# SSD group-norm factors: broadcast to all partitions by two DMAs through DRAM in place of products with the identity

## The chip, the core and the metric

The kernel runs on one core of one Trainium2 chip. The metric is the device time of one execution in microseconds (us). Three executions of the kernel before took 2750.94, 2751.69 and 2755.02 us; their median is 2751.69 us.

## The reference

The program is a two-layer decoder trunk on 1040 positions (16 learned meta tokens and 1024 inputs) of width 1024. Layer 0 mixes with an RG-LRU and an S5, layer 1 with a Mamba-2 SSD; each is followed by a squared-ReLU MLP. The change lies in the SSD mixer of layer 1, in the norm over each of its 8 groups of 256 channels:

```python
def ssd_mixer(h, w_in, conv_w, conv_b, dt_bias, a_log, d, norm_w, w_out):
    proj = h @ w_in
    z = proj[..., :SSD_INNER]
    ...
    y = ssd_chunked(xs, dt, a, bm, cm) + d.astype(jnp.float32)[:, None] * xs
    g = y.reshape(bsz, t, SSD_INNER) * jax.nn.silu(z.astype(jnp.float32))
    g = g.reshape(bsz, t, SSD_GROUPS, -1)
    g = g * lax.rsqrt(jnp.mean(g * g, axis=-1, keepdims=True) + NORM_EPS)
    g = g.reshape(bsz, t, SSD_INNER) * norm_w.astype(jnp.float32)
    return g.astype(dtype) @ w_out
```

## The kernel before

Activations are held with channels on the 128 partitions and tokens on the free axis, in three token tiles: 384, 384 and 256 tokens in the SSD's output (`TL`), and 16 more in the first one ahead of it. Every large product is made of three TensorE passes on parts of the operands (`mm3`, L182 to L184), into PSUM tiles `mm`, of which there are 4; small products go to 4 PSUM tiles `sm`.

The SSD stage works on the 8 groups one after the other (`mixer1`, loop over g). For each group it runs over 9 chunks of tokens, c from 0 to 8. `ssd_s1` transposes a chunk (L1358), makes the score product (L1372) and turns a loaded decay tile `csb` into weights (L1376 on ACT, L1378 on POOL); `ssd_s2` makes the chunk's output in an `mm` tile (L1389, L1392) and the next state (L1396), and DVE finishes the output into `zs` (L1412 to L1418). Between the steps of a chunk TensorE is given other products: the input projections of the next group (`proj`: evacuated by ACT at L1267, then by DVE at L1264, L1272 and L1274, or L1285 to L1290 for the gates) and the output projections of earlier token tiles (`wout`: DVE adds each result to `h`, L1471).

After the chunks 3, 6 and 8 the token tile i = 0, 1 or 2 is complete, and `ssd_norm` (L1421) is added to a list of generators that `step` moves on. It has these parts:

- ACT squares both halves of the tile, POOL adds them.
- `token_sums`: for each chunk of 128 tokens a product with a column of ones (L253) leaves the sums with tokens on partitions, and DVE makes the factor 1/sqrt(mean + eps) by a bit trick and three Newton steps (L258, L193 to L198). The result is `rsy`, 128x3 for a tile of 384 tokens and 128x2 for one of 256; its last step is an L198.
- `token_bcast` (L270): for each chunk a product of the factors with the identity writes them to all partitions, on the free axis, in the `sm` tile. Each of these products stands as two rows in the trace. There are 3 of them for i = 0 and 1, and 2 for i = 2, 8 a group.
- DVE multiplies both halves of `zs` by the norm's weights and the factors (L1443), ACT casts the result to `yh` (L1455), DVE makes the rest `yl` (L1456). `yh` and `yl` are what `wout` multiplies.

The engines work each in the order of their own queue. That order is set when the program is built, by a scheduler that takes instructions by priority as their inputs become ready; the table `SHIFT` (L64) shifts the priority of some functions, in this stage of `token_sums` and `load_w`. SP's queue issues the DMAs of the stage in its order: weights `wraw` (three buffers), decay tiles `csb` and `ecb` (three buffers each).

Of the kernel before, what the change touches and what calls it, by code (L numbers as in the profile page):

```python
# [10 lines left out]
F32 = mybir.dt.float32  # L11
# [7 lines left out]
P = 128  # L19
# [59 lines left out]
class Trunk:  # L79
# [1341 lines left out]
    def ssd_norm(self, pg, g, i):  # L1421

        nc = self.nc
        v = nc.vector
        o, w = TL[i]
        y = self.prod[g, "z", i]
        m = o - TT[i][0]
        acc, sq = (self.prod[g, k, i][:, m:m + w] for k in ("x0", "x1"))
        nc.scalar.activation(out=acc, in_=y[:, 0], func=AF.Square)
        nc.scalar.activation(out=sq, in_=y[:, 1], func=AF.Square)  # L1430
        nc.gpsimd.tensor_tensor(out=acc, in0=acc, in1=sq, op=ALU.add)
        yield
        yield
        sums = self.token_sums([acc], w, 256, self.sm())
        yield
        if i == 0:
            self.flush()
            self.wo[g] = [self.load_w(self.A["ssd_out"][2 * g + j], pg, "o", lo_pool=(j == 1)) for j in range(2)]
        wo = self.wo[g]
        yield  # L1440
        rb = self.token_bcast(sums, w)
        for j in range(2):
            v.scalar_tensor_tensor(out=y[:, j], in0=y[:, j], scalar=self.col("gnorm", 2 * g + j), in1=rb, op0=ALU.mult, op1=ALU.mult)  # L1443
        if g == 7 and i != 1:

            pool, q, wt = ((self.px, "xbc0", 400), None, (pg, "xbc1", 384))[i]
            yh, yl = ([pool.tile([P, wt], F32R, name=q, bufs=6) for _ in range(2)] for _ in range(2))
            for j in range(2):
                nc.scalar.copy(yh[j][:, :w], y[:, j])
                v.tensor_tensor(out=yl[j][:, :w], in0=y[:, j], in1=yh[j][:, :w].bitcast(F32), op=ALU.subtract)  # L1450
        else:
            self.flush(8)
            yh = pg.tile([P, 2, 384], F32R, name="yh", bufs=2)
            yl = pg.tile([P, 2, 384], F32R, name="yl", bufs=2)
            nc.scalar.copy(yh[:, :, :w], y)  # L1455
            v.tensor_tensor(out=yl[:, :, :w], in0=y, in1=yh[:, :, :w].bitcast(F32), op=ALU.subtract)  # L1456
            yh, yl = ([q[:, j] for j in range(2)] for q in (yh, yl))
        yield
        self.wq += [(g, wo, (yh, yl), i, n) for n in range(KT)]
# [252 lines left out]
```

## Time and profile before

| | |
|---|---|
| median of three executions | 2751.69 us |
| the profiled execution | 2751.07 us |
| its span in the trace | 2749.3 us |
| TensorE (PE) busy, whole span | 2664.6 us, 97% |
| VectorE (DVE) busy | 1963.5 us, 71% |
| ScalarE (ACT) busy | 1076.9 us, 39% |
| GpSimd (POOL) busy | 1034.7 us, 38% |
| SSD stage with its eight groups | 1163 to 2060 us of the span |

The profiled execution stands 0.6 us under the median of the runs. Times of instructions are read from its trace, in us from the start of the span. A busy PE is a pipelined one: its rows overlap, and the cost of a row is the time from its start to the start of the next one. Idle time of an engine that isn't the bound costs nothing by itself.

### The profile page before, as it was taken

How to read it: one execution, taken by the hardware profiler on the slowest of the kernel's cores; microseconds unless marked ns; L12 is line 12 of the kernel's file. 1: busy time of each engine (PE TensorE's matmuls, PEld its weight loads, DVE VectorE, ACT ScalarE, POOL GpSimd, SP SyncE). 2: the span in 40 equal slices, each digit the busy share in tenths (PEclk: the TensorE clock that was granted, in tenths of full speed). 3: DMA queues.
4: the chain of work that ended last, by engine and by line, in shares of the span. 5: the costliest groups of instructions: out<-in, count | busy, mean ns of one | idle time of the engine just before them, and what ended most of it. 6: DMA issues, size and time to landing. Idle time of an engine off the chain costs nothing.

```text
span 2749.3 us, 44507 instructions
## 1 busy us (share of the span) xinstructions
PE 2664.6 (97%) x17121; PEld 2551.6 (93%) x17121; DVE 1963.5 (71%) x3877; ACT 1076.9 (39%) x2207; POOL 1034.7 (38%) x842
## 2 busy tenths in 40 slices
PE   7998999999999999999999999999989999999998
PEld 7887999999999999899999999998988999999998
DVE  9887465666666686876767767677786666666685
ACT  5565344233233233453434434344454333333334
POOL 2122115454444532142233322333444554554542
PEclk9989999999999999999999999999999999999999
DMA  4422411111111110121211212123311111111111
GB/s 165 112 76 57 148 47 47 47 54 43 51 51 47 51 39 29 44 94 59 69 62 60 76 59 69 62 60 97 109 55 64 54 51 50 54 50 50 47 43 62
DMA packets 117909, 176.35 MB, mean 64 GB/s; under 512 B 13376, under 2 KB 47936, under 8 KB 117568
## 3 DMA queue, kind: packets, MB, share of 16 engines
q1 hardware_dynamic: 117408, 173.34, 20.3%
q8 instruction: 135, 2.21, 0.3%
q14 instruction: 78, 0.64, 0.1%
q10 hardware_dynamic: 288, 0.15, 0.0%
HBM read 158.34 MB, written 8.72 MB: 61 GB/s over the span
## 4 chain that ended last, share of the span: by engine, by line
PE 51%; DVE 6%; ACT 1%; DMA 1%; POOL 1%; issue 0%; DVEq 0%; ACTq 0%; POOLq 0%; SPq 0%
PE mm L182 12%; PE mm L183 12%; PE mm L184 12%; PE pd L182 3%; PE pd L184 3%; PE pd L183 3%; DVE xbc L1272 1%; PE mm L1392 1%; PE sm L1396 1%; PE mm L1389 1%; PE sm L1358 1%; DMA csb<-csd 1%; PE sm L253 1%; PE sm L270 0%; PE sm L1372 0%
## 5 line engine op out<-in xcount | busy, mean ns | idle before, releaser
L182 PE MATMUL mm<-hi,whi 128*128 128x384 f32 (+4 forms) x3120 | 1019.0, 327 | 16.1 <-ACT whi L176 8.6
L183 PE MATMUL mm<-lo,whi 128*128 128x384 f32 (+4 forms) x3120 | 1007.5, 323 | 0.9 <-DVE lo L300 0.5
L184 PE MATMUL mm<-hi,wlo 128*128 128x384 f32 (+4 forms) x3120 | 1004.2, 322 | 2.3 <-POOL wlo L177 2.3
L182 PEld LDWEIGHTS mm<-hi,whi 128*128 128x128 f32 x3120 | 591.0, 189 | 26.0 <-ACT whi L176 9.4
L183 PEld LDWEIGHTS mm<-lo,whi 128*128 128x128 f32 x3120 | 590.9, 189 | 7.2 <-DVE lo L300 0.8
L184 PEld LDWEIGHTS mm<-hi,wlo 128*128 128x128 f32 x3120 | 592.5, 190 | 3.3 <-POOL wlo L177 3.0
L182 PE MATMUL pd<-pc 128*128 128x260 f32 (+1 forms) x1176 | 377.0, 321 | 6.3 <-DVE s L375 2.2
L184 PE MATMUL pd<-pc 128*128 128x260 f32 (+1 forms) x1176 | 374.7, 319 | 0.0
L183 PE MATMUL pd<-pc 128*128 128x260 f32 (+1 forms) x1176 | 373.6, 318 | 0.0
L492 DVE TENSOR_TENSOR h<-h,pd 128x520 f32<-128x520 f32 (+1 forms) x336 | 291.8, 870 | 59.6 <-PE pd L184 45.2
L375 DVE SCALAR_TENSOR_TENSOR s<-mm,rb 128x384 f32<-128x384 f32 (+2 forms) x192 | 98.6, 514 | 265.1 <-PE mm L184 252.2
L389 POOL TENSOR_TENSOR pc<-ca,pc 128x512 fp32r<-128x512 f32 x112 | 169.8, 1516 | 244.8 <-ACT pc L388 164.1
L389 POOL TENSOR_TENSOR pc<-draw,pc 128x512 fp32r<-128x512 f32 x84 | 125.1, 1489 | 338.2 <-ACT pc L388 338.2
L182 PEld LDWEIGHTS pd<-pc 128*128 128x128 f32 x1176 | 221.5, 188 | 22.1 <-DVE acc L492 4.5
L184 PEld LDWEIGHTS pd<-pc 128*128 128x128 f32 x1176 | 221.6, 188 | 15.9
L183 PEld LDWEIGHTS pd<-pc 128*128 128x128 f32 x1176 | 221.6, 188 | 12.5
L176 ACT CAST whi<-wraw 128x512 fp32r<-128x512 f32 x286 | 167.6, 616 | 164.1 <-PE mm L183 150.2
L376 ACT ACTIVATE sq<-s 128x384 f32<-128x384 f32 (+2 forms) x192 | 94.1, 490 | 347.1 <-DVE s L375 347.0
L492 DVE TENSOR_TENSOR acc<-acc,pd 128x520 f32<-128x520 f32 (+1 forms) x234 | 190.3, 861 | 4.2 <-PE pd L184 4.1
L177 DVE TENSOR_TENSOR wlo<-wraw,whi 128x512 fp32r<-128x512 f32 x224 | 167.0, 764 | 18.1 <-ACT whi L176 9.4
L1378 POOL TENSOR_TENSOR csb<-csb,sc 128x512 f32<-128x512 f32 x64 | 89.7, 1402 | 210.3 <-DVE sc L1374 199.1
L388 ACT CAST pc<-cb 128x520 fp32r<-128x520 f32 (+1 forms) x112 | 70.0, 625 | 247.2 <-PE pd L184 130.4
(390 smaller groups left out, 4531.6 us busy)
## 6 DMA issues: line engine op xcount, KB each, us to landing
wraw<-in_mlp_up SPq DMA_DIRECT2D x128, 256.0 KB
wraw<-in_ssd_in SPq DMA_DIRECT2D x120, 256.0 KB
draw<-in_mlp_down SPq DMA_DIRECT2D x112, 256.0 KB
csb<-csd SPq DMA_DIRECT2D x64, 256.0 KB
ecb<-ecd SPq DMA_DIRECT2D x128, 64.0 KB
wraw<-in_ssd_out SPq DMA_DIRECT2D x32, 256.0 KB
wraw<-in_ev_in SPq DMA_DIRECT2D x24, 256.0 KB
wraw<-in_ev_out SPq DMA_DIRECT2D x18, 256.0 KB
```

The costliest lines, as they stand in the source:

```text
L176: nc.scalar.copy(h, raw)
L177: e.tensor_tensor(out=l, in0=raw, in1=h.bitcast(F32), op=ALU.subtract)
L182: nc.tensor.matmul(pt, lhsT=whi, rhs=xhi, start=first, stop=False)
L183: nc.tensor.matmul(pt, lhsT=whi, rhs=xlo, start=False, stop=False)
L184: nc.tensor.matmul(pt, lhsT=wlo, rhs=xhi, start=False, stop=last)
L253: nc.tensor.matmul(st[:l, 508 + i:509 + i], lhsT=a[:, o:o + l], rhs=self.ones, start=j == 0, stop=j == len(accs) - 1)
L375: nc.vector.scalar_tensor_tensor(out=r, in0=pt[:, :w], scalar=0.0, in1=rbs[i], op0=ALU.max, op1=ALU.mult)
L376: nc.scalar.activation(out=dst[:, o - t0:o - t0 + w].bitcast(F32), in_=r, func=AF.Square)
L388: nc.scalar.copy(hi, x)
L389: e.tensor_tensor(out=lo, in0=x, in1=hi.bitcast(F32), op=ALU.subtract)
L492: v.tensor_tensor(out=d, in0=d, in1=src, op=ALU.add)
L1378: nc.gpsimd.tensor_tensor(out=csb, in0=csb, in1=sc.unsqueeze(1).broadcast_to([P, 4, P]), op=ALU.mult)
```

## The change

For the first seven groups the products of `token_bcast` are left out. The factors are stored by one DMA into a tile in DRAM, so that the 128 tokens of a chunk lie one behind the other there (the store's elements are 4 bytes each), and a second DMA reads this row of 384 or 256 factors back into all 128 partitions of an SBUF tile `rbg`, of which there is one. The last group keeps the products. Lines behind L1434 stand 9 lines lower in the changed kernel: L1443 is L1452 there, L1455 is L1464, L1456 is L1465, L1471 is L1480.

```diff
         sums = self.token_sums([acc], w, 256, self.sm())
+        if g < 7:
+
+            st, y1, ch = sums
+            fd = self.dr.tile([3, P], F32, name=f"fd{g}{i}")
+            n = len(ch)
+            nc.sync.dma_start(fd[:n].rearrange("c p -> p c"), y1)
+            rb = pg.tile([P, 384], F32, name="rbg", bufs=1)[:, :w]
+            nc.sync.dma_start(rb, fd[:n].rearrange("c p -> (c p)").unsqueeze(0).broadcast_to([P, w]))
         yield
         if i == 0:
             self.flush()
             self.wo[g] = [self.load_w(self.A["ssd_out"][2 * g + j], pg, "o", lo_pool=(j == 1)) for j in range(2)]
         wo = self.wo[g]
         yield
-        rb = self.token_bcast(sums, w)
+        if g == 7:
+            rb = self.token_bcast(sums, w)
```

SP's queue has 42 more DMAs, 21 stores (L1440) and 21 loads (L1442). In the third group it reads, from the norm of the first tile to that of the third:

```order
L174 DMA wraw<-in_ssd_in 128x512 x2
L1440 DMA fd_15334<-rsy 128x3x1
L174 DMA wraw<-in_ssd_in 128x512 x2
L1442 DMA rbg<-fd_15334 128x384
L1341 DMA csb<-csd 128x512
...
L1344 DMA ecb<-ecd 64x2x128 x2
L1440 DMA fd_15800<-rsy 128x3x1
L174 DMA wraw<-in_ssd_in 128x512
L1442 DMA rbg<-fd_15800 128x384
L174 DMA wraw<-in_ssd_in 128x512
L1341 DMA csb<-csd 128x512
...
L1440 DMA fd_16135<-rsy 128x2x1
L1442 DMA rbg<-fd_16135 128x256
```

For i = 0 and 1 loads of weights stand between the store and the load back; for i = 2 the load back is the next in the queue, and so waits there for the store.

On DVE the products with the factors move forward. In the third group's second norm (i = 1) the queue before reads, from the last evacuation of a projection's tile 2 on:

```order
L1274 SCALAR_TENSOR_TENSOR xbc_15703<-s_15704,xbc_15703 128x256
L1272 SCALAR_TENSOR_TENSOR xbc_15764<-mm,cols,xbc_15764 128x399
L1412 TENSOR_TENSOR ty<-mm,ecb 128x256
...
L1274 SCALAR_TENSOR_TENSOR xbc_15764<-s_15765,xbc_15764 128x400
L1418 TENSOR_TENSOR zs_14956<-zs_14956,ty 128x2x128
L1272 SCALAR_TENSOR_TENSOR xbc_15830<-mm,cols,xbc_15830 128x384 x3
L1264 TENSOR_TENSOR s_15865<-mm,rb_11522 128x260
L1443 SCALAR_TENSOR_TENSOR zs_14803<-zs_14803,cols,sm 128x384 x2
```

and that of the changed kernel, from the same instruction on:

```order
L1274 SCALAR_TENSOR_TENSOR xbc_15712<-s_15713,xbc_15712 128x256
L1452 SCALAR_TENSOR_TENSOR zs_14809<-zs_14809,cols,rbg 128x384 x2
L1465 TENSOR_TENSOR yl<-zs_14809,yh 128x768
L1272 SCALAR_TENSOR_TENSOR xbc_15773<-mm,cols,xbc_15773 128x399
L1412 TENSOR_TENSOR ty<-mm,ecb 128x256
```

The two products and the rest `yl` now stand ahead of the evacuation of the first tile of the next projection. In the third norm (i = 2) they move in the same way, from behind the L1418 of the last chunk to ahead of the L1374:

```order
L1290 SCALAR_TENSOR_TENSOR zs_16112<-s_16113,zs_16112 128x384
L1480 TENSOR_TENSOR h<-h,mm 128x384 x2
L1452 SCALAR_TENSOR_TENSOR zs_14966<-zs_14966,cols,rbg 128x256 x2
L1465 TENSOR_TENSOR yl<-zs_14966,yh 128x2x256
L1374 TENSOR_TENSOR sc<-sm,tri 128x128
```

In the first norm (i = 0) the products stand some three instructions earlier. TensorE's queue is the same up to the end of the seventh group but for the products that are left out; there some 64 of its instructions change places.

## Rows read from the trace of the kernel before

**Rows 1.** The page, busy time of TensorE over the span.
```profile
PE 2664.6 (97%) x17121; PEld 2551.6 (93%) x17121; DVE 1963.5 (71%) x3877; ACT 1076.9 (39%) x2207; POOL 1034.7 (38%) x842
```
**Rows 2.** Busy time by windows: span, then busy us of each engine, PEclk, DMA.
```profile
1424.00:1538.00 114.00, 113.69 (x767) 109.38 (x766) 82.21 (x202) 46.38 (x108) 35.75 (x34) 1.00 0.22 65
```
**Rows 3.** Waits of PE, 1200 to 1960: us in total, times, longest.
```profile
PE mm L1389 <- DVE h L1471: 4.6, 6, 1.5
...
PE mm L183 <- DVE yl L1456: 0.8, 4, 0.3
```
**Rows 4.** Line L270, 1160 to 2060: duration ns, and who waited for it.
```profile
L270 PE MATMUL sm<-ident,rsy x134: 270/275/421, 1221.1 to 2048.5; 128*128 128x128 f32 x134
...
  DVE zs L1443: 11.5, 13
```
**Rows 5.** Timeline of PE, third group, i = 1: start, us, instruction.
```profile
1488.19 0.83 PE L270 MATMUL sm<-ident,rsy 128*128 128x128 f32 x6
1488.86 0.49 PE L1358 MATMUL sm<-ident,xbc 128*16 128x128 f32 x3
1489.10 0.42 PE L182 MATMUL mm<-hi,whi 128*128 128x384 f32 x1
```
**Rows 6.** Timeline of PE, third group, i = 2.
```profile
1523.38 0.61 PE L270 MATMUL sm<-ident,rsy 128*128 128x128 f32 x4
1523.74 0.36 PE L182 MATMUL mm<-hi,whi 128*128 128x256 f32 x1
```
**Rows 7.** Timeline of SP in layer 0: a store to DRAM and its load.
```profile
271.86 2.59 SPq L871 DMA_DIRECT2D yd<-s5yg  x4
276.50 0.33 SPq L877 DMA_DIRECT2D s5y<-yd  x1
```
**Rows 8.** Timeline of ACT in layer 0: the first reader of that load.
```profile
279.81 0.95 ACT L884 ACTIVATE s<-s5y 128x400 f32<-128x400 f32 x2 [0.49 <-DMA s5y<-yd]
```
**Rows 9.** The page, DMA queues: packets, MB, share of 16 engines.
```profile
q1 hardware_dynamic: 117408, 173.34, 20.3%
```
**Rows 10.** Timeline of SP, third group, around the norms i = 0 and 1.
```profile
1437.14 6.54 SPq L174 DMA_DIRECT2D wraw<-in_ssd_in  x4
...
1474.99 3.18 SPq L174 DMA_DIRECT2D wraw<-in_ssd_in  x2
```
**Rows 11.** Timeline of DVE, third group, i = 1; in brackets the idle time before.
```profile
1473.83 0.16 DVE L198 SCALAR_TENSOR_TENSOR rsy<-rst,rsy 128x3 f32<-128x3 f32 x1
...
1477.73 0.42 DVE L1274 SCALAR_TENSOR_TENSOR xbc<-s,xbc 128x256 f32<-128x256 f32 x1
1480.74 0.63 DVE L1272 SCALAR_TENSOR_TENSOR xbc<-mm,cols,xbc 128x399 f32<-128x399 f32 x1 [2.59 <-ACT xbc L1267]
...
1483.70 0.90 DVE L1274 SCALAR_TENSOR_TENSOR xbc<-s,xbc 128x400 f32<-128x400 f32 x1 [0.41 <-ACT s L1273]
...
1486.66 1.93 DVE L1272 SCALAR_TENSOR_TENSOR xbc<-mm,cols,xbc 128x384 f32<-128x384 f32 x3 [1.73 <-ACT xbc L1267]
```
**Rows 12.** Timeline of DVE, third group, i = 2.
```profile
1509.46 0.16 DVE L198 SCALAR_TENSOR_TENSOR rsy<-rst,rsy 128x2 f32<-128x2 f32 x1
...
1512.24 0.55 DVE L1471 TENSOR_TENSOR h<-h,mm 128x384 f32<-128x384 f32 x1 [0.16 <-PE mm L184]
1517.02 0.29 DVE L1374 TENSOR_TENSOR sc<-sm,tri 128x128 f32<-128x128 f32 x1 [4.22 <-PE sm L1372]
```
**Rows 13.** Timeline of DVE, third group, i = 0.
```profile
1441.04 0.15 DVE L198 SCALAR_TENSOR_TENSOR rsy<-rst,rsy 128x3 f32<-128x3 f32 x1
...
1450.03 1.92 DVE L1272 SCALAR_TENSOR_TENSOR xbc<-mm,cols,xbc 128x384 f32<-128x384 f32 x3
```
**Rows 14.** Line L1443, 1160 to 2060: duration ns min/median/max.
```profile
L1443 DVE SCALAR_TENSOR_TENSOR zs<-zs,cols,sm x48: 473/605/615, 1222.7 to 2049.2; 128x384 f32<-128x384 f32 x32, 128x256 f32<-128x256 f32 x16
```
**Rows 15.** Line L1272 with operands in SBUF alone, 1160 to 1960.
```profile
L1272 DVE SCALAR_TENSOR_TENSOR xbc<-s,cols,xbc x78: 462/478/1516, 1160.5 to 1836.5; 128x256 f32<-128x256 f32 x78
```
**Rows 16.** Busy time by windows, in the last group's tail.
```profile
1998.80:2012.50 13.70, 11.05 (x44) 9.13 (x44) 11.21 (x33) 5.05 (x13) 5.85 (x7) 0.50 0.09 28
```

## The prediction

> **What bounds the kernel now.** I read the page first. TensorE is busy for 97% of the span and no other engine comes near it [rows 1]: read from this row that DVE, ACT and POOL have a fourth or more of the time to spare on average. Then I read windows of one group of the SSD stage each, since an average says nothing of a stage. In the third group's window TensorE is busy 113.69 of 114.00 us at a granted clock of 1.00 (the upper level, 2.4 GHz), DVE 82.21 [rows 2]. So here a product that is left out shortens the path, as long as nothing else becomes late. The waits of TensorE say the same: its largest, for DVE's additions to `h`, are 4.6 us in six places over 760 us, and those for the rest `yl` are 0.8 us [rows 3]. Last I read the places of the change on TensorE, DVE and SP.
>
> **What is removed.** The trace has 134 rows of L270 in the stage, about 275 ns each [rows 4]. They overlap, so I price them by starts. At i = 1 the three products are six rows from 1488.19, and the next instruction starts at 1488.86: 0.67 us [rows 5]. At i = 2 the two products start at 1523.38 and the next instruction at 1523.74: 0.36 us [rows 6]. With i = 0 like i = 1, a group loses 2 x 0.67 + 0.36 = 1.70 us, and seven groups lose **11.9 us**. The L1443 behind them waited for L270 for 11.5 us [rows 4], but on DVE, which has time; I count nothing for that.
>
> **What is added: the two DMAs.** Their landing is not in the trace of before, so I bound it. The nearest row is the bounce in layer 0, where 128-partition rows are stored to `yd` and loaded back. Four stores take 2.59 us to issue from 271.86, so the last begins near 273.9; the load is issued at 276.50, 2.6 us later [rows 7]; its first reader starts at 279.81, 3.3 us later, having waited for that DMA [rows 8]. One bounce is then 2.6 + 3.3 = **5.9 us** from the factors to the readers. This is the low end. The change stores single elements of 4 bytes, 384 of them. The page gives 117408 packets on the main queue at 20.3% of 16 engines over 2749.3 us [rows 9], so 0.203 x 16 x 2749.3 / 117408 = 0.076 us for a packet of 1.5 KB on average. If each element is a packet and they are spread over 16 engines, 24 packets add 1.8 us (7.7 us in all); if one engine takes them all, 29 us are added (35 us in all). I take 5.9 to 7.7, since the same queue spreads all its other work, and keep 35 as the far end. The Trainium skill ("DMA: Bandwidth & Descriptors", section "Rules for kernel authors") speaks against such a store: a non-contiguous last dimension is lowered to one descriptor per element, and should be rearranged. No row here shows a store of that kind; by that rule the bounce is the 7.7 or the 35 above, not the 5.9.
>
> **What the bounce delays.** *SP.* At i = 0 and 1 the queue has weight loads around these moments (1437.14 for 6.54 us, 1474.99 for 3.18 us [rows 10]), and the new order puts one or two between store and load back, which covers most of the store's landing. What stands behind, `csb`, comes later by two issues of about 0.33 us each [rows 7]; TensorE has no wait for `csb` among those above 0.3 us. I count nothing.
>
> *DVE, i = 0.* Factors at 1441.2, DVE at the products near 1450.0 [rows 13]: 8.8 us, more than 7.7. No wait.
>
> *DVE, i = 1.* Factors at 1474.0. The moved L1452 stands behind the L1274 that ends at 1478.15. DVE was idle there for 2.59 us anyway, until 1480.74 [rows 11]. With 5.9 us `rbg` lands at 1479.9: DVE waits 1.8 us. Then come two products (0.605 us each [rows 14]), ACT's cast and DVE's rest. These two are as wide as both products together; I take 1.2 us each. So the evacuation of the next projection tile (L1272) starts at 1479.9 + 3.6 = 1483.5 in place of 1480.74, 2.8 us late. DVE's gaps of 0.41 and 1.73 us right behind [rows 11] take 2.1 us of it. TensorE doesn't feel it before it needs that tile's `mm` buffer again. There are four: this tile, the output tile of the chunk, the next two projection tiles; the fifth begins at 1489.10 [rows 5]. The tile's readers were done by 1483.3 (the start of L1274 less its gap of 0.41 [rows 11]), so 5.8 us of delay are free. **The limit:** L1272 may start at 1486.5, `rbg` may land at 1482.9, and the bounce may take 8.9 us.
>
> *DVE, i = 2.* Factors at 1509.6, DVE at the moved products at 1512.8; it idled 4.22 us there, until 1517.02 [rows 12]. With 5.9 us `rbg` lands at 1515.5. Products, cast and rest on two thirds of the width take 2.4 us, so the L1374 at 1517.02 starts 0.9 us late. I assume the limit of i = 1 here too. In return `yl` is ready some ten microseconds before `wout` wants it, so the 0.8 us of waits for it [rows 3] may go.
>
> *DVE's own time.* L1443 read PSUM and now reads SBUF alone. Such an L1272 of 256 columns takes 478 ns in the median, as L1443's shortest (473), but up to 1516 [rows 14, 15]. The cost over 42 instructions lies between nothing and 42 x 1.0 = 42 us, near the median by far, on an engine idle for 32 of 114 us a group. It is hidden by those gaps; without them it would be TensorE's.
>
> **Sum.** The profiled execution took 2751.07 us, 0.6 under the median of the runs. 2751.07 - 11.9 = 2739.2; against the median 2739.8. I forecast **2740 us**.
>
> **Rivals.**
> 1. *The gain is given back in small waits or in the tail.* For: late evacuations at i = 1 end within 0.7 us of what the gaps take; TensorE already waits for DVE's L1471 six times [rows 3]; in the end of the seventh group some 64 instructions of TensorE change places; and the last group has a stretch of 13.70 us at a granted clock of 0.50 (the lower level, 1.2 GHz), in which TensorE was busy 11.05 us [rows 16]. Were that stretch half as long again, 13.7 / 2 x 0.5 = 3.4 us would go; 0.5 us at each of 14 norms gives back 7. Together 10.4, or a time near 2750; with either alone 2743 to 2747. Against: the four `mm` buffers. Within 0.2% (5.5 us) of before, 2746 to 2757: 17%.
> 2. *Slower: the element store makes the bounce longer than the limit.* DVE stands still in its queue at L1452, no `mm` tile is evacuated, and TensorE stops. Each microsecond over 8.9 costs up to one at each of the 14 norms with i = 1 and 2. The change loses from 8.9 + 11.9 / 14 = 9.8 us on. A bounce of 12 us gives 3.1 x 14 - 11.9 = +31, 2783 us; one engine for all elements (35 us) would give 26.1 x 14 - 11.9 = +353, 3105 us. For: no row shows so fine a store. Against: 384 elements are little work when spread. 12%. The skill's rule above is this rival's first step: by it alone, with the packets spread, the sum stays.
> 3. *More gain.* DVE's norm work moves forward, PSUM's `sm` tile is free sooner, and TensorE's waits of 4.6 and 0.8 us [rows 3] vanish: 2740 - 5.4 = 2734.6 us. Part of the faster cases, 12%.
> 4. *The removed products were hidden.* If TensorE had been waiting at those places, nothing would be gained. The rows before and behind are back to back [rows 5, 6], so I give it no share of its own beyond the first rival.
>
> **How the numbers follow.** About 0.2% is what a measurement of this kernel can tell from no change. Forecast with its near misses (2736 to 2746): 59%; more gain: 12%; so faster 71%, same 17%, slower 12%. The range leaves out the slower rival and the far end of the others: 2734 (all waits gone) to 2750 (both give-backs).
>
> **What would show it.** Right: 112 rows of L270 fewer in the stage; a group's period shorter by 1.7 us; DVE waits of one to three microseconds for `rbg` at i = 1 and fewer or none at i = 0; no new wait of TensorE above a microsecond. Wrong: from the readiness of the factors to the start of L1452 more than 9 us; new waits of TensorE for L1272 or L1471 at i = 1 or 2; SP late with `csb`, seen as waits of TensorE for POOL's L1378; a longer stretch at 0.50 in the last group.

## The result and the profile after

The changed kernel took 2918.59 us (median of five executions, 2915.51 to 2921.41) beside 2751.6 us before: a ratio of 1.0606, with a 95% interval of 1.0594 to 1.0617. It is **167 us slower** where 12 us less were forecast. The profiled execution has a span of 2913.8 us. One of the eight executions of e15 below took 6615.55 us in a slower state and is left out of its time.

The page of the changed kernel: busy time, then the chain of work that ended last by engine and by line.

```profile
PE 2693.8 (92%) x17009; PEld 2574.2 (88%) x17009; DVE 1974.7 (68%) x3877; ACT 1078.2 (37%) x2207; POOL 1040.6 (36%) x842
...
PE 36%; DVE 11%; DMA 11%; ACT 2%; issue 1%; POOL 1%; SPq 0%; ACTq 0%; DVEq 0%; POOLq 0%
PE mm L182 8%; PE mm L183 8%; PE mm L184 8%; DMA fd<-rsy 7%; PE pd L182 3%; PE pd L184 3%; PE pd L183 3%; DVE xbc L1272 2%; DMA rbg<-fd 2%; DMA csb<-csd 1%; DVE xbc L1274 1%; DVE rst L197 1%; PE sm L1396 1%; DVE zs L1452 1%; DVE rst L196 1%
```

TensorE has fallen from 97% [rows 1] to 92%, and the chain now runs through DMAs for 11% of the span, 7% of it the store `fd`. TensorE is also *busy* 29 us longer, though it has fewer instructions. The next view, one group of the stage in a window of 139.90 us, shows both parts (columns as in rows 2):

```profile
1393.10:1533.00 139.90, 119.04 (x748) 113.64 (x749) 84.74 (x202) 46.63 (x107) 36.92 (x34) 0.93 0.23 57
```

A group now takes 140.3 us in place of 114.3 (mean of five, from one `csb` load to that of the next group). TensorE idles 20.9 us of it, where it idled 0.3 [rows 2], and is busy over 5 us longer because its granted clock is 0.93. The mean hides two levels, as windows around one of its waits show:

```profile
1507.00:1511.20 4.20, 0.00 (x0) 0.00 (x0) 1.46 (x3) 2.35 (x6) 0.00 (x0) 1.00 0.27 70
1511.20:1518.00 6.80, 4.55 (x12) 3.67 (x12) 6.76 (x11) 2.94 (x6) 3.61 (x2) 0.50 0.24 72
```

First TensorE has nothing to do for 4.2 us; then, while it still waits, it is granted half its clock (0.50, the level of 1.2 GHz) for 6.8 us. There are about 20 us at 0.50 in each group; before there were none in these five groups.

What TensorE waits for in the stage (1160 to 2240), us in total, times, longest:

```profile
PE sm L1358 <- DVE xbc L1274: 45.1, 8, 7.9
PE mm L182 <- DVE xbc L1272: 34.8, 6, 6.8
PE mm L182 <- ACT zs L1289: 26.4, 7, 4.6
PE mm L182 <- DVE ty L1414: 20.1, 6, 3.5
```

These are evacuations and the steps just behind them, 126 us in all; the largest such sum in rows 3 was 4.6. DVE and SP in the same stretch:

```profile
DVE zs L1452 <- DMA rbg<-fd: 172.8, 21, 10.9
```

```profile
SPq L1442 <- DMA fd<-rsy: 164.0, 21, 9.7
```

DVE stands before each of the 21 products, SP before each load back. One bounce in SP's timeline, at i = 0 of the third group, and its reader in that of DVE:

```profile
1491.96 0.38 SPq L1440 DMA_DIRECT2D fd<-rsy  x1
1492.44 1.98 SPq L174 DMA_DIRECT2D wraw<-in_ssd_in  x2
1501.44 0.33 SPq L1442 DMA_DIRECT2D rbg<-fd  x1
1501.86 0.38 SPq L1341 DMA_DIRECT2D csb<-csd  x1
```

```profile
1500.42 0.42 DVE L1418 TENSOR_TENSOR zs<-zs,ty 128x256 f32<-128x256 f32 x1 [0.62 <-POOL ty L1416]
1507.44 0.62 DVE L1452 SCALAR_TENSOR_TENSOR zs<-zs,cols,rbg 128x384 f32<-128x384 f32 x1 [6.60 <-DMA rbg<-fd]
```

From store to load back 9.5 us pass, and 6.0 more to the product. Over the 21 norms the bounce from the factors to the product takes 12.7 to 16.1 us, 14.1 in the mean: the store alone 8.1 to 11.3 from its issue to its landing, the load back 3.3 to 6.0 to the product. Of the signs that the prediction named, L270 has 112 rows fewer as foreseen (102 in the whole trace in place of 214), but the bounce is over 9 us and TensorE waits for L1272.

### The profile page after: what moved, and what is told of

Its sections match the earlier page's. It is cut to its first block, busy times and chain, and to the rows that moved or that the text cites. A ratio compares the mean times of both kernels' runs of the same rounds, so it can differ in the third digit from the quotient of the medians.

```text
span 2913.8 us, 44394 instructions
## 1 busy us (share of the span) xinstructions
PE 2693.8 (92%) x17009; PEld 2574.2 (88%) x17009; DVE 1974.7 (68%) x3877; ACT 1078.2 (37%) x2207; POOL 1040.6 (36%) x842
## 4 chain that ended last, share of the span: by engine, by line
PE 36%; DVE 11%; DMA 11%; ACT 2%; issue 1%; POOL 1%; SPq 0%; ACTq 0%; DVEq 0%; POOLq 0%
PE mm L182 8%; PE mm L183 8%; PE mm L184 8%; DMA fd<-rsy 7%; PE pd L182 3%; PE pd L184 3%; PE pd L183 3%; DVE xbc L1272 2%; DMA rbg<-fd 2%; DMA csb<-csd 1%; DVE xbc L1274 1%; DVE rst L197 1%; PE sm L1396 1%; DVE zs L1452 1%; DVE rst L196 1%
## 5 line engine op out<-in xcount | busy, mean ns | idle before, releaser
L182 PE MATMUL mm<-hi,whi 128*128 128x384 f32 (+4 forms) x3120 | 1032.9, 331 | 72.0 <-ACT zs L1289 25.6
L183 PE MATMUL mm<-lo,whi 128*128 128x384 f32 (+4 forms) x3120 | 1021.5, 327 | 0.9 <-DVE lo L300 0.5
L184 PE MATMUL mm<-hi,wlo 128*128 128x384 f32 (+4 forms) x3120 | 1016.6, 326 | 2.0 <-POOL wlo L177 2.0
L182 PEld LDWEIGHTS mm<-hi,whi 128*128 128x128 f32 x3120 | 603.3, 193 | 86.3 <-ACT zs L1289 28.0
L183 PEld LDWEIGHTS mm<-lo,whi 128*128 128x128 f32 x3120 | 602.8, 193 | 7.1 <-DVE lo L300 0.8
L184 PEld LDWEIGHTS mm<-hi,wlo 128*128 128x128 f32 x3120 | 604.2, 194 | 3.9 <-POOL wlo L177 3.7
L1378 POOL TENSOR_TENSOR csb<-csb,sc 128x512 f32<-128x512 f32 x64 | 90.0, 1406 | 260.8 <-DVE sc L1374 249.6
```

The lines of the kernel that those rows point to most:

```text
L182: nc.tensor.matmul(pt, lhsT=whi, rhs=xhi, start=first, stop=False)
L183: nc.tensor.matmul(pt, lhsT=whi, rhs=xlo, start=False, stop=False)
L184: nc.tensor.matmul(pt, lhsT=wlo, rhs=xhi, start=False, stop=last)
L1378: nc.gpsimd.tensor_tensor(out=csb, in0=csb, in1=sc.unsqueeze(1).broadcast_to([P, 4, P]), op=ALU.mult)
```

## The experiments

Each ratio is against runs of the kernel before on the same chip.

**What the products were worth.** The DMAs go too; the multiplication reads a column of factors that is already in SBUF.

```diff
-            nc.sync.dma_start(fd[:n].rearrange("c p -> p c"), y1)
-            nc.sync.dma_start(rb, fd[:n].rearrange("c p -> (c p)").unsqueeze(0).broadcast_to([P, w]))
+            rb = sums[1][:, :1].broadcast_to([P, w])
```

> In the first seven groups neither the products with the identity nor the DMAs are there: the second operand of the multiplication is the first column of the factors, read with a step of 0 (the wrong factor for most tokens). If the removal is worth what was summed (11.9 us), this takes about 2740 us (2735 to 2746). If the removed products had been hidden, it takes 2750 or more.

2740.38 us, ratio 0.9957 (0.994 to 0.9973). The removal is worth 12.3 us (7 to 17 by the interval); the sum had 11.9.

**DMAs that nobody reads.** DVE's order is that of before but for one pair of instructions, SP's that of the change.

```diff
-        if g == 7:
-            rb = self.token_bcast(sums, w)
+        rb = self.token_bcast(sums, w)
```

> The products with the identity are back and feed the multiplication; the two DMAs stay in SP's queue, and nothing reads what they bring. Theory A (the loss is DVE standing still at the multiplication until the bounce has landed): within 6 us of before, 2748 to 2758, although SP waits for the store as long as in the changed kernel. Theory C (the loss is SP's queue, held up by the load back that waits for the store, so that decay tiles and weights come late): 2890 to 2935.

2864.27 us, ratio 1.0407 (1.0391 to 1.0423). Both expectations missed: 112 us are lost without DVE ever waiting for the bounce, so standing at L1452 is not the whole loss, and not most of it. TensorE waits for casts and evacuations, ACT for decay tiles; first the waits of TensorE, then that of ACT, then ACT's in the kernel before:

```profile
PE mm L182 <- ACT yh L1463: 43.0, 8, 8.1
PE sm L1396 <- DVE xte L1365: 25.0, 8, 5.0
```

```profile
ACT csb L1376 <- DMA csb<-csd: 248.1, 42, 11.5
```

```profile
ACT csb L1376 <- DMA csb<-csd: 152.6, 36, 8.2
```

So the decay tiles were loads that ACT already stood waiting for before the change. In the changed kernel this wait is 183.2 us, beside 159.1 for the products of L1452.

**An earlier decay tile.**

```diff
-        csb = pool.tile([P, 4, P], F32, name="csb", bufs=3)
+        csb = pool.tile([P, 4, P], F32, name="csb", bufs=4)
...
-        ecb = pool.tile([P, 2, P], F32, name="ecb", bufs=3)
+        ecb = pool.tile([P, 2, P], F32, name="ecb", bufs=4)
```

> As e2_spare (products kept, DMAs in SP's queue, nothing reads them), but with four buffers for the decay tiles csb and ecb in place of three, so that a decay tile is loaded one chunk earlier. Theory C1 (SP's queue stands at the load back until the store has landed; the decay tile behind it comes late; ACT, in order, stands at L1376, and with it the evacuations behind): most of the 112 us of e2_spare go, 2745 to 2775. Theory C2 (it is the weights, or the traffic of the small elements itself): 2840 to 2870.

> The changed kernel with four buffers for csb and ecb. What is left is DVE standing at the multiplication. If DVE's wait alone makes the whole loss (A), 2900 to 2920. If SP's hold makes it (C1), 2740 to 2760. If both stand one beside the other and each is enough by itself, 2840 to 2900.

2860.01 us (1.039, 1.0374 to 1.0405) and 2910.88 us (1.0575, 1.056 to 1.0591). Neither tells anything: the scheduler left `csb` behind the load back in SP's queue, and SP waited for L1392 ahead of it for 257.7 us as in e2 (257.6). The edit didn't do what it was meant to.

**Store and load without the wait between them.**

```diff
-            nc.sync.dma_start(rb, fd[:n].rearrange("c p -> (c p)").unsqueeze(0).broadcast_to([P, w]))
+            nc.sync.dma_start(rb, self.csd[0, :n].rearrange("c p -> (c p)").unsqueeze(0).broadcast_to([P, w]))
```

> The changed kernel, but the second DMA reads a row of the decay table that has long been in DRAM in place of the factors just stored (wrong factors). Store, load and all their bytes stay; neither SP nor DVE waits for the store any more. If the loss is waits alone: 2735 to 2748, as e1_drop. If the traffic of the 4-byte elements itself costs: 2780 or more.

2850.25 us, ratio 1.0353 (1.0336 to 1.0371). Neither SP nor DVE waits for the store, and still 110 us are lost against e1. (The scheduler also gave DVE's queue another order here: the products stand one to two chunks earlier than in the changed kernel.) SP's timeline around one store, the next L1376 of ACT, and the same L1376 in the kernel before:

```profile
1475.79 0.38 SPq L1440 DMA_DIRECT2D fd<-rsy  x1
1476.27 1.98 SPq L174 DMA_DIRECT2D wraw<-in_ssd_in  x2
1478.35 0.38 SPq L1341 DMA_DIRECT2D csb<-csd  x1
```

```profile
1489.86 1.28 ACT L1376 ACTIVATE csb<-csb,cs 128x128 f32<-128x128 f32 x4 [9.05 <-DMA csb<-csd]
```

```profile
1447.06 1.29 ACT L1376 ACTIVATE csb<-csb,cs 128x128 f32<-128x128 f32 x4 [0.81 <-DMA csb<-csd]
```

`csb` is issued 2.6 us behind the store and lands 11.4 us later; `csb` loads of the kernel before land 3.3 us after their issue in the median (3.0 to 4.8). **What is issued behind the store lands after it:** 44 loads of e7 were issued with at least 3.3 us left before a store landed, and none landed before that store. ACT works in order, so it stands at L1376 with casts and evacuations behind it, and TensorE runs out of buffers; these last two links are read from the waits. SP's own wait (theory C1 of e5) isn't needed for this.

**Is it the queue?**

```diff
-            nc.sync.dma_start(fd[:n].rearrange("c p -> p c"), y1)
+            nc.scalar.dma_start(fd[:n].rearrange("c p -> p c"), y1)
```

> As e7_no_dependence (wrong factors, nobody waits for the store), but ACT's queue issues the store of the 4-byte elements in place of SP's. If its elements hold up only what is issued behind them on the same queue: loads on SP land in their 2.5 to 3.3 us again, 2736 to 2755. If they hold up the 16 DMA engines themselves: 2830 to 2860.

2825.87 us, ratio 1.0272 (1.0255 to 1.0289): 4 us short of the second range, and far from the first. SP's loads come late behind ACT's store as well: one `csb` is issued at 1505.14, 6.7 us after the store, and is waited for until 1512.21.

```profile
1512.21 1.28 ACT L1376 ACTIVATE csb<-csb,cs 128x128 f32<-128x128 f32 x4 [4.49 <-DMA csb<-csd]
```

The queues share what the store holds. This fits the Trainium skill ("DMA: Bandwidth & Descriptors", section "Issuing engines are not separate DMA queues"): transfers of all issuing engines run on the same 16 DMA engines.

**What makes the store slow: number or place.** The first edit stores 128 elements, the second all of them, 64 bytes apart; e14 and e15 have 4 and 8 in place of 16. On each of the five engines these four kernels have the instructions of e7 in the order of e7, so that they differ in the store alone.

```diff
-            nc.sync.dma_start(fd[:n].rearrange("c p -> p c"), y1)
+            nc.sync.dma_start(fd[:1].rearrange("c p -> p c"), y1[:, :1])
```

```diff
-            fd = self.dr.tile([3, P], F32, name=f"fd{g}{i}")
+            fd = self.dr.tile([3, P, 16], F32, name=f"fd{g}{i}")
...
-            nc.sync.dma_start(fd[:n].rearrange("c p -> p c"), y1)
+            nc.sync.dma_start(fd[:n, :, 0].rearrange("c p -> p c"), y1)
```

> As e7_no_dependence (the load back reads a row of the decay table, so the factors are wrong and nobody waits for the store), but the store takes only the first column of the factors: 128 elements of 4 bytes in place of 384 or 256. If the hold of the queue goes by the number of elements, loads issued behind the store land some 3 us later than usual in place of 4 to 8, and the time falls to 2755 to 2790. If it is a fixed price of a store with 4-byte elements, 2840 to 2855.

> As e7_no_dependence (wrong factors, nobody waits for the store), but the 384 (256) elements lie 64 bytes apart in DRAM in place of one behind the other. If it is the number of elements: 2840 to 2860, as e7. If neighbours in DRAM hinder each other: the store lands in 2 to 5 us and the time falls to 2735 to 2780.

> As e10_spread (wrong factors, nobody waits for the store), the elements 16 bytes apart in DRAM. If elements must be 64 bytes apart to be cheap: the store lands in 5 to 9 us and the time is 2800 to 2850. If any gap between them is enough: 1.6 to 2.5 us and 2752 to 2760.

> As e14, the elements 32 bytes apart. If 64 bytes are needed: landing between that of e14 and e10, time 2770 to 2830; if 32 are enough, 1.6 to 2.2 us and 2752 to 2760.

| 4-byte elements | apart | store lands after (median) | time, us | ratio (95%) |
|---|---|---|---|---|
| 384, 256 (e7) | 4 B | 9.2 us | 2850.25 | 1.0353 (1.0336 to 1.0371) |
| 128 (e9) | 4 B | 7.8 us | 2832.07 | 1.0295 (1.028 to 1.031) |
| 384, 256 (e14) | 16 B | 2.7 us | 2758.99 | 1.0025 (1.0012 to 1.0038) |
| 384, 256 (e15) | 32 B | 1.9 us | 2755.04 | 1.0015 (1.0005 to 1.0026) |
| 384, 256 (e10) | 64 B | 1.8 us | 2756.52 | 1.0016 (1.0007 to 1.0025) |

A third (or half) of the elements saves only 1.4 us of landing; a gap of 12 bytes saves 6.5, and a gap of 60 bytes takes 94 us off the time. **The price is in elements that lie directly beside one another in DRAM, hardly in their number.** (e9's time lies between its two ranges, nearer the fixed price; e14's store landed just behind its range.) e10 still takes 16 us more than e1. It has two more DMAs for each norm and another order of DVE's queue, and which of them costs this was not tried.

The traces' records of single DMA packets show where the store spends its time. In e7 and in e10 alike each element is a packet of 4 bytes with a record of 9 ns, and all begin 0.9 to 1.2 us after the store's issue (medians). The landing follows 7.9 us later in e7 and 0.5 us later in e10. In between, the packets of the large loads are held: of those of 2048 bytes from 1160 to 2060 (84 ns in the median), 238 took over 1 us in e7 (8.7 us at most), 4 in e10 and one before.

At i = 0 of the third group SP's queue reads in e10 as above in e7, with `csb` again 2.6 us behind the store; but ACT begins on it 4.4 us after its issue, in place of 11.5 (the view names POOL, the load landed 0.1 us before):

```profile
1444.07 0.38 SPq L1440 DMA_DIRECT2D fd<-rsy  x1
1444.55 1.99 SPq L174 DMA_DIRECT2D wraw<-in_ssd_in  x2
1446.63 0.38 SPq L1341 DMA_DIRECT2D csb<-csd  x1
```

```profile
1451.02 1.28 ACT L1376 ACTIVATE csb<-csb,cs 128x128 f32<-128x128 f32 x4 [1.93 <-POOL H L1402]
```

The rule that the prediction weighed, one descriptor per element (the Trainium skill, "DMA: Bandwidth & Descriptors", section "Rules for kernel authors"), agrees with the traces of e7 and e10: each has 7840 packets of 4 bytes more than that of the kernel before, 7168 for the elements of 21 stores and 16 for each of 42 DMAs. But it is no price by itself: in e10 384 elements landed in under 2 us.

**Longer runs.** A partition's factors as one run; DVE reads the row with a step. e4 transposes them with one product first, e17 starts the runs every 16 bytes.

```diff
-            nc.sync.dma_start(fd[:n].rearrange("c p -> p c"), y1)
+            nc.sync.dma_start(fd, y1)
...
+            rb = rb.rearrange("q (p c) -> q c p", c=n)
```

```diff
+            nc.tensor.transpose(st[:n, :P], y1, self.ident)
+            fr = self.tp.tile([3, P], F32, name="fr")
+            v.tensor_copy(fr[:n], st[:n, :P])
...
-            nc.sync.dma_start(fd[:n].rearrange("c p -> p c"), y1)
+            nc.sync.dma_start(fd[:n], fr[:n])
```

> The factors are stored with the partition outermost, so that a partition's 3 (2) factors are one run of 12 (8) bytes: 128 runs in place of 384 (256) elements; DVE reads the row back with a step of 3 (2). Theory A1 (the store is slow by the number of its separate elements): it lands 3 to 6 us after its issue in place of 8 to 11, and the time falls to 2760 to 2840. Theory A2 (any store to DRAM from here takes so long, whatever its elements): landing 8 to 11 us, 2905 to 2930.

> The factors are first transposed by one product (128x3 to 3x128) and copied to SBUF by DVE; the store then has 3 (2) runs of 512 bytes. Theory A1: the store lands 1.5 to 3 us after its issue, the bounce takes 6 to 8 us, and the time is 2740 to 2775. Theory A2: landing 8 to 11 us, 2905 to 2930.

> As e3_run12 (a partition's 3 or 2 factors as one run), but the runs begin every 16 bytes in a DRAM tile that is filled once at the stage's start; the load back brings 512 words, of which DVE reads each fourth (and its 2 or 1 neighbours). If it is pieces that share 16 bytes with a neighbour that are slow: the store lands in 1.6 to 2.7 us in place of 3.7, and the time is that of e13, 2753 to 2764. If runs of 12 bytes are slow by themselves: 3.5 us or more and 2770 to 2785.

The stores land in 3.7, 1.1 and 1.4 us (medians); the times are 2781.18 (1.0102, 1.0087 to 1.0117), 2762.73 (1.0043, 1.0028 to 1.0059) and 2766.33 us (1.0056, 1.0043 to 1.0069). Theory A2 of e3 is out; theory A1, by the number of elements, fits e3's range but not e9. From e3 to e17 the same runs, moved to a pitch of 16 bytes, land 2.3 us sooner; e17's time missed its range by 2 us.

**The change's own waits with a short store.** As e10, but the load back reads the tile just stored (one tile for all norms, filled once), and DVE's and TensorE's queues have the order of the changed kernel.

```diff
-            nc.sync.dma_start(rb, fd[:n].rearrange("c p -> (c p)").unsqueeze(0).broadcast_to([P, w]))
+            nc.sync.dma_start(rb, fd[:n].rearrange("c p s -> (c p s)")[:w].unsqueeze(0).broadcast_to([P, w]))
```

> The changed kernel with its own waits (SP's for the store, DVE's for the load back) and DVE's order as changed, but the elements are stored 64 bytes apart, into one DRAM tile that is filled once at the stage's start; the load back reads the tile's first 384 (256) words, so most factors are wrong. The store lands in 1.6 to 2.2 us here, so the bounce is 5 to 6 us, which is what the prediction was summed with. If the size of the bounce (and what the store holds up) was the only step that failed: 2738 to 2748. If waits remain that the sum hadn't: 2752 to 2770.

2759.71 us, ratio 1.0033 (1.002 to 1.0045). With the elements apart, the changed kernel gets back 159 us. Here the bounce is what the forecast was summed with, 4.5 to 5.9 us at i = 1 and 2 of the first six groups: at i = 1 of the third group the store is issued at 1476.55, the load at 1478.26, and DVE waits 1.00 us for it (1.8 was foreseen). The first two lines of DVE are from i = 0, the last from i = 1.

```profile
1476.55 0.38 SPq L1440 DMA_DIRECT2D fdx<-rsy  x1
...
1478.26 0.32 SPq L1442 DMA_DIRECT2D rbg<-fdx  x1
```

```profile
1451.48 1.66 DVE L1274 SCALAR_TENSOR_TENSOR xbc<-s,xbc 128x384 f32<-128x384 f32 x1
1453.06 1.51 DVE L1272 SCALAR_TENSOR_TENSOR xbc<-s,cols,xbc 128x256 f32<-128x256 f32 x1
...
1481.67 1.15 DVE L1452 SCALAR_TENSOR_TENSOR zs<-zs,cols,rbg 128x384 f32<-128x384 f32 x2 [1.00 <-DMA rbg<-fdx]
```

At i = 1 and 2 no wait of TensorE over 2 us is left. But the time is 20 us over the forecast, and TensorE's timeline has the place, at i = 0, once in each of five groups:

```profile
1458.84 0.66 PE L182 MATMUL mm<-hi,whi 128*128 128x388 f32 x1 [3.55 <-DVE ty L1414]
```

There DVE works from 1447.34 to 1458.70 without a gap, and some of its instructions are two to three times as long as usual (1.66 and 1.51 above; the first took 0.55 at its place before, and 0.48 is the median of the second [rows 15]). POOL is at its own casts then:

```profile
1450.65 3.63 POOL L177 TENSOR_TENSOR wlo<-wraw,whi 128x512 fp32r<-128x512 f32 x2 [3.69 <-ACT whi L176]
```

That the one slows the other was not tried alone, but the trace of the kernel before bears it out. Of the 78 instructions of [rows 15], the 54 with no work of POOL beside them all took 462 to 487 ns; the 17 over 990 ns all had POOL at work for at least 0.72 of their time. Four of the five waits are followed by 3.4 or 6.8 us at half the clock.

**Products held back.** A scalar operand that DVE copies late was to keep the multiplications at about their places of before (e8 on e3 and with the buffers of e5, e12 on e4 and with the transposing product one step later); e16 stores to one SBUF row first, then to DRAM, then back.

```diff
+            yield
+            zn = self.prod[g, "z", i + 1] if i < 2 else self.prod[g + 1, "z", 0]
+            gc = pg.tile([P, 2], F32, name="gc", bufs=2)
+            v.scalar_tensor_tensor(out=gc, in0=zn[:, 0, :1].broadcast_to([P, 2]), scalar=0.0, in1=self.col("gnorm", 2 * g, 2), op0=ALU.mult, op1=ALU.add)
```

```diff
+            nc.sync.dma_start(fs.rearrange("o (p c) -> o p c", c=n), y1)
+            nc.sync.dma_start(fd, fs)
```

> e3_run12 (store in runs of 12 or 8 bytes) with four buffers for csb and ecb, and with DVE's two multiplications held back: their scalar operand is a copy of the norm's weights that DVE makes after the product of the next chunk (one more DVE instruction of 128x2 for each norm), so that they stand in DVE's queue where they stood before the change. If waits are all there is, the bounce of 7 to 9 us is hidden: 2738 to 2748. If something else of the bounce costs, 2765 to 2780.

> e4_row512 (one transposing product, store in runs of 512 bytes) with the transposing product one step later, and the multiplications held back as in e8 by a scalar operand that DVE copies after the next chunk's gate. If only the waits at L1452 and for the factors separated e4_row512 from before: 11.9 us less two thirds of the products put back as one (21 products of about 0.25 us, 5 us): 2742 to 2750. If other waits take their place: 2755 to 2770.

> The factors are stored in runs of 12 (8) bytes into one partition's row in SBUF, that row goes to DRAM as one piece, and the load back follows as in the change; DVE reads it with a step of 3 (2) as in e3_run12. If it is writes beside one another in DRAM that are slow, each hop lands in 1 to 2 us, the load back in 3 to 4, 6 to 8 us in all, nothing holds the queue, and the multiplications stand at about their places of before: 2740 to 2749, under both kernels. If small writes to SBUF are as slow: 2775 or more.

2774.2 (1.0079, 1.0064 to 1.0094), 2772.83 (1.0078, 1.0059 to 1.0096) and 2769.04 us (1.0067, 1.0054 to 1.0079): all slower than before. e8 came out in its second range, but it held nothing back: DVE makes the copy 2.2 us behind the store's issue at the latest, the products stand as early as in the changed kernel or earlier, and DVE waits for `rbg` for 57.7 us (47.3 in e3). So it doesn't test its question. In e12 the products do stand at their places of before or a little later, and DVE waits for `rbg` for only 8.7 us; its time is above both ranges, and TensorE's waits are many and small (9.5 us the largest sum). What costs there stays open. In e16, between its ranges, the store to SBUF landed in 2.0 us, so it was quick, but three hops are long: DVE waits for `rbg` for 20.7 us. TensorE's waits moved to other evacuations (27.2 us for `h` in e8, 20.4 for L1414 in e16).

**The bounce for two tiles out of three.** e17, with the products kept for i = 0.

```diff
-        if g < 7:
+        if g < 7 and i:
...
-        if g == 7:
+        if g == 7 or i == 0:
             rb = self.token_bcast(sums, w)
```

> As e17_pitch16, but with the bounce for the token tiles 1 and 2 alone; tile 0, where e13 still shows a wait of TensorE of 3.4 us in each group, keeps its three products. It saves 7 x (0.67 + 0.36) = 7.2 us of products: 2741 to 2748 if nothing else waits, faster than both kernels; 2750 to 2760 if another wait takes the place.

2744.29 us, ratio **0.9976 (0.9967 to 0.9985)**: faster than both kernels, and 7.4 us (0.24%) faster than before, where 7.2 were summed. The window of rows 2 for this kernel:

```profile
1424.00:1538.00 114.00, 113.75 (x766) 109.47 (x765) 83.63 (x202) 47.21 (x110) 35.62 (x34) 1.00 0.23 70
```

TensorE is as full as before and its clock stays at 1.00; a group takes 113.0 us in place of 114.3.

## Why the prediction was wrong

- **The removal, 11.9 us: right.** e1 measured 12.3, and e18 7.4 for the 7.2 of two tiles; TensorE was indeed the bound there.
- **The bounce, 5.9 to 7.7 us: the step that failed.** It was 12.7 to 16.1. The 2.6 us for the store were 8.1 to 11.3. The analogue of rows 7 and 8 stores runs of 520 bytes, and the surcharge for elements was priced by the mean packet of rows 9. Neither row holds a store of neighbouring 4-byte elements. Each element was a packet, as weighed, but all of them began within 0.3 us; the price lies between the last packet and the landing, a term that the sum didn't have. The far end of 35 us was kept as a bound but not in the range.
- **"csb ... I count nothing": the second failure.** The sum charged the DMAs with their own latency and SP's issues, and never asked what else lands late while the store is under way. It looked for `csb` among TensorE's waits alone, while ACT already waited 152.6 us for it. For the same reason its sign for a late `csb`, waits of TensorE for POOL's L1378, came to 1.4 us in all. e7 loses 110 us without any wait for the bounce, of the 179 that the change loses (167 and the 12 of the products). The other 69 come with the waits for the bounce; since e7 also has another order on DVE and the two causes overlap, this is no exact split. What both have in common is the store: with its elements apart, 159 of the 179 are gone (e13).
- **"DVE, i = 0 ... No wait": wrong with the bounce.** DVE waits 6.2 to 8.5 us there in the first six groups.
- **The second rival** was the right one in kind: the bounce passes its limit, DVE stands at L1452, TensorE stops. Its point of decision (9.8 us) was passed. Its price was far too small: by its formula a bounce of 14.1 us costs 5.2 x 14 - 11.9 = +61 us, where +167 were measured; the norms with i = 0, the late decay tiles and the clock weren't in it. It had 12%, and the range left it out.
- **The clock** was a term for the last group alone. In the changed kernel it fell during or after nearly every wait of TensorE of 3.3 us and more, about 20 us at 0.50 in each group.
- **"DVE's own time ... hidden by those gaps": wrong at one place.** With the bounce as short as assumed (e13) the forecast still misses by 20 us. An average of 32 free us in a group [rows 2] hid that DVE has none for 11 us at i = 0, where TensorE is only just behind it. At i = 1 and 2 the step held, as e13 and e18 show. TensorE's five waits there come to 17.0 us; how far the 16 us that e10 loses are among the 20 was not separated.

## What to carry to other kernels

Price a new DMA by what it does to the transfers behind it, not by its own latency and issue alone: look for the loads that an engine already waits for, and for what stands behind them in its queue, not only at the waits of the engine that is the bound. Choose the analogue by the form of the write; a store of separate small elements is told by rows of such a store or not at all, and where there are none its far end belongs in the range. When a bounce is needed, keep neighbouring small pieces apart in DRAM (16 bytes were enough here), and use it only where the consumer has a gap that is long at that place, not on average.

## What the runs showed of the hardware

- 128 neighbouring 4-byte elements stored to DRAM landed 7.8 us after the issue (e9), 384 or 256 after 9.2 (e7); the same took 2.7 us at a distance of 16 bytes (e14) and 1.8 at 64 (e10). In e7 and e10 the packets began equally early; only the landing was late. Runs of 12 (8) bytes took 3.7 us end to end (e3), and 1.4 with a pitch of 16 (e17). Stored to one partition's row in SBUF, end to end, they took 2.0 (e16). Why neighbours hinder each other, and why the price hardly grows from 128 to 384, stays open.
- While such a store is under way, other loads land late, whichever engine issued the store: `csb` up to 12.8 us after its issue in e7 and 11.9 in e11, where 3.3 us are the median before.
- In the changed kernel nearly every wait of TensorE of 3.3 us and more had 3.4 or 6.8 us at a granted clock of 0.50 in it or behind it, so a wait cost more than its length; in e13 four of five such waits had. The waits of up to 1.5 us for L1471 before [rows 3] had not.
- A multiplication of DVE with its operands in SBUF (128x256) took 0.46 to 0.49 us with POOL idle, and up to 1.52 with POOL at work beside it (the kernel before).
